# The delta rule's solve emitted in 12 steps between halves of a stream's weights, and the retention's gates directly behind the retention

## The chip, the cores and the metric

The kernel runs on one core of a Trainium2 chip. The metric is device time in microseconds (us) from the start to the end of one execution; the median of three executions is used. A profile of one execution shows what each engine did: PE (matmuls), PEld (its weight loads), DVE (vector engine), ACT (scalar engine), POOL, and the DMA queues, of which SP issues all that matter here.

## The reference

One layer on 256 rows of width 2048, in float32: a mixer of two branches, cross-attention into 256 memory rows, an MLP. The mixer is where the change lies. All its inputs are columns of one product `h @ w_in`:

- Retention, 8 heads: q and k with rotary angles, scores times a decay, scores times v, a group norm, then `silu(rg) * yr`.
- Delta rule, 16 heads in chunks of 64: q, k, v through a short causal convolution and silu; then

```
m = where(strict, (k*beta) @ k.T * decay, 0)
t = triangular_solve(eye + m, eye)      # the elimination
u = t @ (v*beta);  w = t @ (k*beta*exp(cum_g))
v_new = u - w @ state                   # the solve, chunk after chunk
o = (q*exp(g)) @ state + (q @ k.T * decay) @ v_new
```

  followed by a norm of each head and `silu(gz) * yg`.
- The merge: `sigmoid(gate_a) * yr + sigmoid(gate_b) * yg`, then `@ w_out`.

So each branch has a silu gate and a sigmoid gate, four blocks of columns of `w_in`: RG and TA for the retention, GZ and TB for the delta rule.

## The kernel before

Every float32 product with weights is made of three products of rounded parts: a weight piece is fetched as 1 MB (`raw`, three buffers), and for each half of it (512 KB) ACT makes the rounded part `whi` (L95) and DVE the rest `wlo` (L96), three buffers each. A "half" below is such a half of a fetch. `blocks` (L174, L175) produces two blocks of 128 feature rows from two fetches, `chunk` (L136 to L138) a piece of 512 columns from four fetches. Both leave their result in PSUM, and a function given by the caller takes it out.

The mixer works in four groups of two retention heads and four delta-rule heads. `gdn_stream` computes q, k and v of a group's four heads, two heads at a time: three `blocks` with convolutions, then the gram matrices (L562 to L566) and the decayed matrices `alt`, the compact blocks `cmp_l` and the right sides `r4`. `gdn_core` has two parts. The elimination: `cmp_l` goes through DRAM (`scr_l`) into `lw`, 31 pairs of small DVE operations on 32 partitions (L619 product, L621 subtraction) invert it into `tw`, which goes through DRAM (`scr_t`, L623) and comes back in four pieces as `ct` (L626); DVE transposes it into `cu` (L628) and makes the block matrices `t` and `u` (L636, four operations each). The solve: 16 small matmuls (L646) make `am`; then nine products of eight 128x128 float32 matmuls each (L653), of which each needs the one before it, taken out of PSUM by ACT (`w`, L665; `y`, L668) or combined by DVE (`sq`, L666 and L667; `r`, L663); at the end the outputs (L677 to L680) and their norm into `yg` (L687).

`retention` computes q and k (two `blocks`), v (a `chunk`), the scores (L720, L721), their products with v (L106 to L108) and the normed `yr`. `gates` runs the chunks RG, TA (on `yr`), GZ, TB (on `yg`) and transposes the merge (L221).

The groups are chained by the loop at the end of the mixer: stream of group j, gates of group j-1, retention of group j, elimination and solve of group j. Nothing else is written out by hand: a scheduler goes through the program with an estimate of durations and places each instruction in its engine's queue by its place in the program's text, moved ahead by `tc.high_priority` (the fetches, and the taking out of PSUM), once its inputs and buffers are there. After that each engine runs its queue in order. Two pairs of PSUM banks (`s0`, `s1`) serve the weights, four banks (`b`) all else. `alt` has four buffers, one for each head of a group, `cmp_l` and `r4` one, and so the next group's first pair can take its gram matrices out only when the solve has read its own.

## Time and profile before

| | us |
|---|---|
| median of 3 executions | 2127.54 |
| lowest, highest | 2123.79, 2130.27 |
| the profiled execution | 2124.05 |
| its span, first to last instruction | 2122.3 |
| PE busy in it | 2088.8 |
| DVE busy | 1409.7 |
| ACT busy | 1091.6 |
| POOL busy | 29.7 |

The profile's page gives the whole, and the trace behind it can be asked for any stretch. In a row of the timeline stand the start, the duration, the engine, the line of the kernel, the operation and what it writes and reads; in square brackets the idle time of the engine before it and who ended it. In a row of the stretches stand its bounds, its length and then the busy time of PE, PEld, DVE, ACT and POOL with their numbers of instructions, the granted clock of PE as a share, the share of DMA and GB/s. The ends of matmuls are modelled, so that a short wait of PE behind a matmul can be shown as busy.

In time, the mixer's stretch goes from about 230 us to about 1125 us. The four eliminations end at 380.5, 509.8, 731.5 and 951.6 us, and the four solves (first L653 to last L653) stand at 392.5 to 408.9, 578.5 to 621.7, 801.3 to 844.5 and 1026.4 to 1077.3 us.

### The profile page before, as it was taken

Reading aid. Unit: us, or ns where it says so; the run is one execution under the profiler, and the core shown is the slowest. Engines: PE = TensorE matmul, PEld = TensorE weight load, DVE = VectorE, ACT = ScalarE, POOL = GpSimd, SP = SyncE. Lnnn points to the kernel's source line nnn. Section 1 sums busy time; section 2 is a strip of 40 time slices with the busy share of each in tenths; the row PEclk is TensorE's granted clock in tenths of the full one; section 3 lists DMA queues with packets and bytes.
Section 4 is the critical chain, followed back from the end, with each engine's and each line's share of the span. In section 5 each row is a group of like instructions: output and inputs, shape, how many; then the busy total and the mean of one; then the engine's idle time right before and its main releaser. Section 6 shows DMA issues by size and latency. Waiting matters only on the chain.

```text
span 2122.3 us, 28778 instructions
## 1 busy us (share of the span) xinstructions
PE 2088.8 (98%) x11172; PEld 1800.5 (85%) x11172; DVE 1409.7 (66%) x2225; ACT 1091.6 (51%) x1700; POOL 29.7 (1%) x39
## 2 busy tenths in 40 slices
PE   8999999799999999999999999999999999999998
PEld 6878888688898889888888899888888888888887
DVE  6756779578667876786557666666556656645655
ACT  7565565354556455645445555554434434434444
POOL 0000000000000000000000000000000000000000
PEclk9999999999999999999999999999999999999999
DMA  8777656355545654455457655566566556556653
GB/s 299 252 237 246 199 186 196 97 181 194 184 144 198 197 185 149 169 196 190 159 173 253 206 182 159 178 198 182 197 197 186 193 196 188 192 198 187 190 198 139
DMA packets 316009, 405.91 MB, mean 191 GB/s; under 512 B 16592, under 2 KB 224480, under 8 KB 315744
## 3 DMA queue, kind: packets, MB, share of 16 engines
q1 hardware_dynamic: 315872, 404.08, 58.9%
q8 instruction: 87, 1.43, 0.3%
q14 instruction: 50, 0.41, 0.1%
HBM read 390.40 MB, written 13.65 MB: 190 GB/s over the span
## 4 chain that ended last, share of the span: by engine, by line
PE 93%; DMA 3%; DVE 1%; ACT 1%; SPq 1%; issue 0%; POOL 0%; ACTq 0%; POOLq 0%; DVEq 0%
PE s L174 32%; PE s L175 16%; PE s L137 13%; PE s L138 13%; PE s L136 13%; PE b L653 2%; DMA row<-crow 1%; DMA xc<-x 1%; DMA dec_d<-dec_w 1%; DVE wlo L96 1%; PE b L564 0%; PE b L106 0%; DMA ct<-scr_t 0%; PE b L108 0%; PE b L107 0%
## 5 line engine op out<-in xcount | busy, mean ns | idle before, releaser
L96 DVE TENSOR_TENSOR wlo<-raw,whi 128x1024 fp32r<-128x1024 f32 x702 | 857.8, 1223 | 507.8 <-ACT whi L95 500.8
L95 ACT ACTIVATE whi<-raw 128x1024 fp32r<-128x1024 f32 x702 | 742.6, 1059 | 715.8 <-PE s L138 373.9
L174 PE MATMUL s<-q,whi 128*128 128x512 f32 x3088 | 1067.4, 392 | 1.2 <-DVE bo L180 0.9
L175 PE MATMUL s<-q,wlo 128*128 128x256 f32 x3088 | 847.3, 282 | 6.6 <-DVE wlo L96 6.6
L174 PEld LDWEIGHTS s<-q,whi 128*128 128x128 f32 x3088 | 573.2, 188 | 112.4 <-DVE bo L180 1.1
L175 PEld LDWEIGHTS s<-q,wlo 128*128 128x128 f32 x3088 | 580.9, 188 | 21.9 <-DVE wlo L96 10.6
L137 PE MATMUL s<-wlo,q 128*128 128x512 f32 x1264 | 494.1, 391 | 0.6 <-DVE wlo L96 0.6
L138 PE MATMUL s<-whi,q 128*128 128x512 f32 x1264 | 491.0, 389 | 0.0
L136 PE MATMUL s<-whi,q 128*128 128x512 f32 x1264 | 449.3, 390 | 0.1
L137 PEld LDWEIGHTS s<-wlo,q 128*128 128x128 f32 x1264 | 237.7, 188 | 49.6 <-DVE wlo L96 1.8
L136 PEld LDWEIGHTS s<-whi,q 128*128 128x128 f32 x1264 | 237.1, 188 | 49.7 <-ACT whi L95 0.5
L138 PEld LDWEIGHTS s<-whi,q 128*128 128x128 f32 x1264 | 237.5, 188 | 48.2
L179 ACT ACTIVATE bo<-s 128x256 f32<-128x256 f32 x193 | 73.0, 378 | 124.7 <-PE s L175 112.6
L180 DVE TENSOR_TENSOR bo<-bo,s 128x256 f32<-128x256 f32 x193 | 80.2, 416 | 47.2 <-ACT bo L179 47.1
L519 DVE SCALAR_TENSOR_TENSOR acc<-bo,cw,acc 128x255 f32<-128x255 f32 (+2 forms) x144 | 66.0, 477 | 2.8 <-ACT acc L516 1.8
L619 DVE TENSOR_TENSOR pr<-lw,tw 32x31 f32<-32x31 f32 (+15 forms) x124 | 40.4, 326 | 10.2 <-DMA lw<-scr_l 8.1
L621 DVE TENSOR_TENSOR tw<-tw,pr 32x31 f32<-32x31 f32 (+15 forms) x124 | 40.6, 328 | 2.5
L945 DVE SCALAR_TENSOR_TENSOR res<-s,rstd3q,res 128x512 f32<-128x512 f32 (+1 forms) x32 | 22.3, 735 | 11.8 <-PE s L138 11.8
L754 ACT ACTIVATE gth<-s 128x512 f32<-128x512 f32 x32 | 18.9, 590 | 18.7 <-PE s L138 15.5
L934 DVE SCALAR_TENSOR_TENSOR hs<-bo 128x256 f32<-128x256 f32 x64 | 27.0, 422 | 1.1
L937 DVE TENSOR_TENSOR q<-hs,q 128x256 fp32r<-128x256 f32 x64 | 26.8, 418 | 0.8 <-ACT q L936 0.8
L936 ACT ACTIVATE q<-hs 128x256 fp32r<-128x256 f32 x64 | 26.2, 410 | 0.0
(292 smaller groups left out, 1083.2 us busy)
## 6 DMA issues: line engine op xcount, KB each, us to landing
raw<-w_in SPq DMA_DIRECT2D x144, 1024.0 KB, 5.0
raw<-w_ff SPq DMA_DIRECT2D x128, 1024.0 KB, 5.4
raw<-w_xkv SPq DMA_DIRECT2D x31, 1024.0 KB, 5.9
raw<-w_out SPq DMA_DIRECT2D x16, 1024.0 KB, 5.8
raw<-w_xq SPq DMA_DIRECT2D x16, 1024.0 KB, 6.7
raw<-w_xo SPq DMA_DIRECT2D x16, 1024.0 KB, 5.3
dec_d<-dec_w SPq DMA_DIRECT2D x16, 192.0 KB, 4.7
dec<-dec_d SPq DMA_DIRECT2D x8, 384.0 KB, 3.2
```

The lines of the kernel that those rows point to most:

```text
L95: act.activation(hi, src, AF.Copy)
L96: vec.tensor_sub(lo, src, hi.bitcast(F32))
L136: pe.matmul(o, xh, wh, start=first, stop=False)
L137: pe.matmul(o, xh, wl, start=False, stop=False)
L138: pe.matmul(o, xl, wh, start=False, stop=last)
L174: pe.matmul(ps[b], lh, xhl, start=kk == 0, stop=False)
L175: pe.matmul(ps[b][:, :S], ll, xh, start=False, stop=kk == KT - 1)
L179: act.activation(o, ps[b][:, S:], AF.Copy)
L180: vec.tensor_add(o, o, ps[b][:, :S])
L519: vec.scalar_tensor_tensor(acc[:, d:], ps[:, :S - d], cw[:, j, blk:blk + 1], acc[:, d:], op0=ALU.mult, op1=ALU.add)
L621: vec.tensor_sub(tw[:, j + 1:32, 0:j + 1], tw[:, j + 1:32, 0:j + 1], pv)
L653: pe.matmul(pv[:, i, :], lhs(i), rhs[:, i, :], start=True, stop=True)
```

## The change

The elimination becomes a function of its own, `gdn_blocks`, called right behind the group's stream. The solve, `gdn_core`, becomes a generator that stops at 12 places: behind `am`, behind each product and its taking out, and behind each of the two outputs. A list `steps` holds the generator that runs. `chunk` and `blocks` call `step()` behind each half of their weights, so that one step of the solve is emitted there; `finish_steps()` empties the list where the next group's first pair needs its buffers. `cmp_l` and `r4` are allocated there instead of at the stream's start. `gates` is split: RG and TA run right behind the group's own retention, GZ and TB stay behind the next group's stream. In groups 1 to 3 the generator is put on the list before RG and TA, so that its steps stand between their halves; in group 0 behind them, so that its steps stand in the next group's stream.

The order of the work: before S0 R0 C0, S1 G0 R1 C1, S2 G1 R2 C2, S3 G2 R3 C3, G3 (S stream, R retention, C elimination and solve, G the four gates); now S0 E0 R0 A0, S1 with the steps of solve 0, E1 B0 R1 A1 with the steps of solve 1, S2 E2 B1 R2 A2 with those of solve 2, S3 E3 B2 R3 A3 with those of solve 3, B3 (E elimination, A the gates RG and TA, B the gates GZ and TB).

```diff
+    steps = []
+
+    def step():
+        if steps and next(steps[0], steps) is steps:
+            steps.pop(0)
+
+    def finish_steps():
+        while steps:
+            step()
...
                     for part in parts:
                         products(q, i, part, halves)
+                    if i % 2:
+                        step()
...
                     pe.matmul(ps[b][:, :S], ll, xh, start=False, stop=kk == KT - 1)
+                if i % (k // 2) == k // 2 - 1:
+                    step()
...
-        cmp_l = mx.tile([P, 8, 32], F32, name="cmp_l", tag="cmp", bufs=1)
-        r4 = mx.tile([P, 4, NT, GD], F32, name="r4", tag="r4", bufs=1)
...
                 blocks(h1, w_in[0], c0 + h0 * GD, 2, evac)
+            if pr == 0:
+                finish_steps()
+                cmp_l = mx.tile([P, 8, 32], F32, name="cmp_l", tag="cmp", bufs=1)
+                r4 = mx.tile([P, 4, NT, GD], F32, name="r4", tag="r4", bufs=1)
...
-    def gdn_core(grp, heads, cmp_l, r4, qe4, yg):
+    def gdn_blocks(heads, cmp_l):
...
+        return t0, u0, am
+
+    def gdn_core(t0, u0, am, heads, r4, qe4, yg):
...
             act.activation(am[:, :, t, :], pv, AF.Copy)
+        yield
...
             if t:
                 vec.tensor_sub(rhs, rhs, times(lambda i: heads[i][:, 0, P:S], y[:, :, 0, :]))
+                yield
             w, sq = tmp("w"), tmp("sq")
             act.activation(w, times(lambda i: am[:, i, t, :], rhs), AF.Copy)
+            yield
             vec.tensor_add(sq, rhs, times(lambda i: am[:, i, t, :], w))
+            yield
             vec.tensor_sub(sq, sq, times(lambda i: am[:, i, t, :], sq))
+            yield
             act.activation(y[:, :, t, :], times(lambda i: u0[:, i, t, :], sq), AF.Copy)
+            yield
...
+        def of_retention(j, yr):
+            chunk(h1, cols(w_in[0], C_RG + 512 * j), silu_gate(yr))
+            chunk(h1, cols(w_in[0], C_TA + 512 * j), sig_gate(yr))
+
+        def of_delta_rule(j, yr, yg, quad, before=None):
+            chunk(h1, cols(w_in[0], C_GZ + 512 * j), silu_gate(yg))
+            chunk(h1, cols(w_in[0], C_TB + 512 * j), sig_gate(yg, yr), before=before)
+            to_feature(lambda t, f: yg[:, t, f * P:(f + 1) * P], None, quad)
...
-            group = gdn_stream(j)
-        if prev is not None:
+            heads, cmp_l, r4, qe4 = gdn_stream(j)
+            solved = gdn_blocks(heads, cmp_l)
+        if j:
...
             else:
+                finish_steps()
                 quad = quad_a()
-            gates(j - 1, prev[0], prev[1], quad, take_back if j == 4 else None)
+            gate_delta_rule(j - 1, yr, yg, quad, take_back if j == 4 else None)
...
             retention(j, yr)
-            gdn_core(j, *group, yg)
-            prev = (yr, yg)
+            core = gdn_core(*solved, heads, r4, qe4, yg)
+            if j:
+                steps.append(core)
+            gate_retention(j, yr)
+            if not j:
+                steps.append(core)
```

Where the instructions now stand is seen in the engines' queues. First PE, in the mixer at the solve of group 0 (`alt` are the group's decayed matrices, `b` a PSUM bank, `s` the PSUM of a weight product, `q` the rows' part). Before:

```order
L174 MATMUL s_4052<-q,whi 128x512
L175 MATMUL s_4052<-q,wlo 128x256
L646 MATMUL b<-alt,t_3420 128x128 x8
L653 MATMUL b<-r_2097,am 128x128 x4
L653 MATMUL b<-w,am 128x128 x4
L653 MATMUL b<-sq,am 128x128 x4
L653 MATMUL b<-sq,u_3421 128x128 x4
L653 MATMUL b<-y,alt 128x128 x4
L653 MATMUL b<-r_2097,am 128x128 x4
```

The same solve on PE now, in three pieces of the queue (L667 was L646, L675 was L653, L187 and L188 were L174 and L175):

```order
L188 MATMUL s_3727<-q,wlo 128x256
L667 MATMUL b<-alt,t_2991 128x128 x8
L187 MATMUL s_3728<-q,whi 128x512
...
L187 MATMUL s_3727<-q,whi 128x512
L675 MATMUL b<-r_2415,am 128x128 x4
L188 MATMUL s_3727<-q,wlo 128x256
...
L187 MATMUL s_3864<-q,whi 128x512
L675 MATMUL b<-w,am 128x128 x4
L188 MATMUL s_3864<-q,wlo 128x256
```

Before, the nine products of group 0's solve stood one behind the other with nothing between; now 23 to 31 rows of weight products stand between two of them. (The program's `x4` and `x8` are twice as many rows in the trace, since each float32 matmul is recorded as two.) In groups 1 and 2 they stood apart by 23 to 29 rows of `blocks` before, and by 22 to 25 of `chunk`, some with `blocks` behind, now; in group 3 by 22 to 27 rows of `chunk` before and 22 to 25 now.

Second DVE, in the mixer at the end of an elimination, here that of group 2, the third (`tw` the inverse, `ct` its way back through DRAM). Before:

```order
L96 TENSOR_TENSOR wlo<-raw,whi 128x1024
L619 TENSOR_TENSOR pr<-lw,tw 32x31
L621 TENSOR_TENSOR tw<-tw,pr 32x31
L96 TENSOR_TENSOR wlo<-raw,whi 128x1024
L613 MEMSET tw 32x1024
L614 MEMSET tw 32x32
L96 TENSOR_TENSOR wlo<-raw,whi 128x1024 x2
L628 STREAM_TRANSPOSE cu<-ct 128x256
L636 TENSOR_TENSOR t_7512<-ct,bd_658 128x256 x4
L636 TENSOR_TENSOR u_7513<-cu,bd_658 128x256 x4
L96 TENSOR_TENSOR wlo<-raw,whi 128x1024 x2
```

The same elimination on DVE now (L107 was L96, L636 and L638 were L619 and L621, L645 was L628, L653 was L636; `st` are the retention's scores, L752 and L753 were L724 and L725):

```order
L107 TENSOR_TENSOR wlo<-raw,whi 128x1024
L636 TENSOR_TENSOR pr<-lw,tw 32x60
L638 TENSOR_TENSOR tw<-tw,pr 32x2x30
L636 TENSOR_TENSOR pr<-lw,tw 32x31
L638 TENSOR_TENSOR tw<-tw,pr 32x31
L752 TENSOR_TENSOR st<-b,dm 128x256
...
L645 STREAM_TRANSPOSE cu<-ct 128x256
L653 TENSOR_TENSOR t_6780<-ct,bd_658 128x256 x4
L752 TENSOR_TENSOR st<-b,dm 128x256
L753 TENSOR_TENSOR st<-b,dm 128x128
L653 TENSOR_TENSOR u_6781<-cu,bd_658 128x256 x4
L107 TENSOR_TENSOR wlo<-raw,whi 128x1024
```

The elimination has moved from the stretch of the four gates to the end of the retention's products, so that its last pairs and the making of `t` and `u` now stand among the retention's scores; three halves' `wlo` stand between its last subtraction and `cu`, as before (four in groups 0 and 1; before three in all but group 3, which had four). The elimination of group 3 stands in the same way.

Third SP, at the way back of the same elimination. Before:

```order
L85 DMA raw<-w_in 128x8x256
L623 DMA scr_t<-tw 32x1024
L626 DMA ct<-scr_t 32x8x32 x2
L85 DMA raw<-w_in 128x8x256
L626 DMA ct<-scr_t 32x8x32 x2
```

Now (L96 was L85, L640 was L623, L643 was L626):

```order
L96 DMA raw<-w_in 128x4x512 x5
L640 DMA scr_t<-tw 32x1024
L643 DMA ct<-scr_t 32x8x32
L96 DMA raw<-w_in 128x4x512
L643 DMA ct<-scr_t 32x8x32 x3
L746 DMA dm<-dm_d 128x256
```

One of the four pieces instead of two is now issued ahead of the next 1 MB of weights, three behind it, in groups 2 and 3; in group 0 it was one and is two, in group 1 it was two and is three. In groups 2 and 3 the decay matrix `dm` of the retention's second head now stands behind the pieces too.

More of the change, by code (lines that the diff above doesn't have):

```diff
@@ L657, in tmp @@
             return mx.tile([P, 4, GD], F32, name=nm, tag="g_" + nm, bufs=1)
-        y = big("y", "g_a")
+        y = mx.tile([P, 4, NT, P], F32, name="y", tag="g_a", bufs=1)
         for t in range(NT):
@@ L688, in gdn_core @@
                                          gdng, op0=ALU.mult, op1=ALU.mult)
+            yield
     def retention(j, yr):
@@ L748, in retention, with gates @@
             vec.tensor_mul(yr[:, t, :], yr[:, t, :], gng)
-    def gates(j, yr, yg, quad, before=None):
+    def gates():
         def gate_of(ps, f, scale):
@@ L769, in sig_gate @@
             return evac
-        chunk(h1, cols(w_in[0], C_RG + 512 * j), silu_gate(yr))
-        chunk(h1, cols(w_in[0], C_TA + 512 * j), sig_gate(yr))
-        chunk(h1, cols(w_in[0], C_GZ + 512 * j), silu_gate(yg))
-        chunk(h1, cols(w_in[0], C_TB + 512 * j), sig_gate(yg, yr), before=before)
-        to_feature(lambda t, f: yg[:, t, f * P:(f + 1) * P], None, quad)
+        def of_retention(j, yr):
[5 more added lines that the diff above has]
+            to_feature(lambda t, f: yg[:, t, f * P:(f + 1) * P], None, quad)
+        return of_retention, of_delta_rule
     kept, merged = [], []
@@ L784, in take_back @@
             merged.append(back)
-    prev = None
+    gate_retention, gate_delta_rule = gates()
     for j in range(5):
         if j < 4:
-            group = gdn_stream(j)
-        if prev is not None:
+            heads, cmp_l, r4, qe4 = gdn_stream(j)
+            solved = gdn_blocks(heads, cmp_l)
+        if j:
             if j < 4:
```

## The prediction

> **What bounds the kernel now.** The page comes first: what share of the span PE works, and what the chain that ended last is made of; its last line here is DVE's conversion of weights, 1.22 us for a half.
>
> ```profile
> span 2122.3 us, 28778 instructions
> PE 2088.8 (98%) x11172; PEld 1800.5 (85%) x11172; DVE 1409.7 (66%) x2225; ACT 1091.6 (51%) x1700; POOL 29.7 (1%) x39
> PE 93%; DMA 3%; DVE 1%; ACT 1%; SPq 1%; issue 0%; POOL 0%; ACTq 0%; POOLq 0%; DVEq 0%
> L96 DVE TENSOR_TENSOR wlo<-raw,whi 128x1024 fp32r<-128x1024 f32 x702 | 857.8, 1223 | 507.8 <-ACT whi L95 500.8
> ```
>
> PE bounds the kernel; the change takes no matmul away, so it can win only time in which PE stands still or runs slowly. Next the stretches of the mixer, to see where PE stands still (the second and third number are length and PE busy).
>
> ```profile
> 240.00:420.00 180.00, 169.17 (x981) 147.81 (x980) 140.12 (x298) 95.56 (x173) 8.95 (x7) 0.99 0.51 163
> 860.00:1080.00 220.00, 220.00 (x1098) 186.63 (x1098) 154.34 (x256) 110.28 (x163) 3.41 (x4) 1.00 0.55 182
> 1080.00:1240.00 160.00, 160.00 (x896) 139.82 (x895) 109.25 (x156) 88.62 (x134) 2.71 (x3) 1.00 0.67 211
> ```
>
> 180.00 less 169.17 is 10.83 us of idle PE in the first row, none in the two others. The mixer's first group has the hole, the later ones have not. The timeline of PE shows what it is:
>
> ```profile
> 394.34 1.16 PE L653 MATMUL b<-w,am 128*128 128x128 f32 x8 [0.69 <-ACT w L665]
> 396.28 1.16 PE L653 MATMUL b<-sq,am 128*128 128x128 f32 x8 [0.78 <-DVE sq L666]
> 416.67 0.39 PE L566 MATMUL b<-kh 128*128 128x256 f32 x1 [1.42 <-DVE yg L687]
> 418.20 0.80 PE L174 MATMUL s<-q,whi 128*128 128x512 f32 x1 [0.92 <-DVE bo L180]
> 418.80 0.41 PE L175 MATMUL s<-q,wlo 128*128 128x256 f32 x1
> 419.01 0.63 PE L174 MATMUL s<-q,whi 128*128 128x512 f32 x1
> 583.60 1.05 PE L653 MATMUL b<-w,am 128*128 128x128 f32 x8
> 584.41 0.36 PE L175 MATMUL s<-q,wlo 128*128 128x256 f32 x1
> 584.97 0.39 PE L174 MATMUL s<-q,whi 128*128 128x512 f32 x1
> 585.20 0.28 PE L175 MATMUL s<-q,wlo 128*128 128x256 f32 x1
> 585.31 0.39 PE L174 MATMUL s<-q,whi 128*128 128x512 f32 x1
> ```
>
> In group 0 each product of the solve waits for the one before it to be taken out: 1.94 us from 394.34 to 396.28. In group 1 the same eight rows cost 0.81 us (583.60 to 584.41), with weight products ahead and behind. And behind group 0's solve a weight product lasts longer: the L174 at 419.01 0.63 us, that at 584.97 0.39. The granted clock says why:
>
> ```profile
> 323.28:432.61 109.33, 98.50 (x575) 85.90 (x574) 83.07 (x181) 52.03 (x99) 6.94 (x5) 0.97 0.44 140
> 561.67:654.42 92.75, 92.75 (x576) 82.97 (x575) 67.20 (x124) 51.37 (x99) 4.41 (x5) 1.00 0.49 158
> 784.45:877.20 92.75, 92.75 (x576) 82.97 (x575) 67.20 (x124) 51.36 (x99) 4.41 (x5) 1.00 0.49 158
> 417.50:424.20 6.70, 6.00 (x19) 5.13 (x20) 6.30 (x19) 4.01 (x14) 1.01 (x1) 0.50 0.18 59
> ```
>
> The last row has a clock of 0.50. The first three are the measure of the whole: each goes from a group's second L721 to the first matmul of the next gates, and holds the same work, the end of the retention, one solve and the next stream (575 and 576 matmuls). It takes 109.33 us around group 0's solve and 92.75 around the two others.
>
> **What the change removes.** Now group 0's products stand 23 to 31 weight rows apart, as in groups 1 and 2 of before, so its stretch should cost what theirs does: 109.33 - 92.75 = 16.6 us less. Of that, 10.83 is idle PE, about 3.0 the half clock (418.2 to 424.2 at half speed does 3.0 us of work), and the rest, some 2.8, waits that modelled ends hide (products shown as busy for 1.16 us that cost 0.81 elsewhere, nine times).
>
> The cover holds: 23 rows are 11.5 pairs of 0.34 us (584.97 to 585.31), 3.9 us; the result needs 0.81 on PE, 0.7 to 0.8 on ACT or DVE (the idle times above), and stands behind at most one conversion of 1.22 us, 2.8 together. Without that cover a product would cost the 1.94 - 0.81 = 1.1 us again.
>
> The moved gates RG and TA are 8 MB of weights with their conversions and taking-out, the same instructions on PE, ACT, DVE and SP at another place. I cost them at nothing: group 3 of before already has RG right behind its own retention and its solve between their halves, and its rows above (860 to 1080, 1080 to 1240) show no idle PE. What waits then is `yr`, at RG's end, eight halves later.
>
> **What it adds: the way back of the elimination.** Before, group 1's to 3's eliminations end during the gates, and `am` follows much later. Now they end just ahead of `am`, among the retention's scores. DVE waits in order at `cu` for `ct`, and behind it stand `wlo` (PE's weights) and, now, `t` for PE's L646. The four waits of before, from the last subtraction to `cu`, and what the third cost:
>
> ```profile
> 380.34 0.18 DVE L621 TENSOR_TENSOR tw<-tw,pr 32x31 f32<-32x31 f32 x1
> 389.18 0.45 DVE L628 STREAM_TRANSPOSE cu<-ct 128x256 f32<-128x256 f32 x1 [0.92 <-DMA ct<-scr_t]
> 509.58 0.18 DVE L621 TENSOR_TENSOR tw<-tw,pr 32x31 f32<-32x31 f32 x1
> 519.27 0.44 DVE L628 STREAM_TRANSPOSE cu<-ct 128x256 f32<-128x256 f32 x1 [1.65 <-DMA ct<-scr_t]
> 731.32 0.18 DVE L621 TENSOR_TENSOR tw<-tw,pr 32x31 f32<-32x31 f32 x1
> 735.41 1.23 DVE L96 TENSOR_TENSOR wlo<-raw,whi 128x1024 fp32r<-128x1024 f32 x1
> 738.13 1.23 DVE L96 TENSOR_TENSOR wlo<-raw,whi 128x1024 fp32r<-128x1024 f32 x1 [1.49 <-ACT whi L95]
> 742.12 0.45 DVE L628 STREAM_TRANSPOSE cu<-ct 128x256 f32<-128x256 f32 x1 [2.77 <-DMA ct<-scr_t]
> 742.49 1.39 DVE L636 TENSOR_TENSOR t<-ct,bd 128x256 f32<-128x256 f32 x4
> 951.38 0.18 DVE L621 TENSOR_TENSOR tw<-tw,pr 32x31 f32<-32x31 f32 x1
> 963.59 0.45 DVE L628 STREAM_TRANSPOSE cu<-ct 128x256 f32<-128x256 f32 x1 [1.46 <-DMA ct<-scr_t]
> 746.41 0.51 PE L175 MATMUL s<-q,wlo 128*128 128x256 f32 x2 [0.77 <-DVE wlo L96]
> 432.61:546.34 113.73, 113.73 (x546) 95.59 (x545) 89.84 (x162) 57.68 (x80) 1.01 (x1) 1.00 0.59 196
> 654.42:769.10 114.68, 113.91 (x546) 95.49 (x545) 88.68 (x160) 56.69 (x79) 1.01 (x1) 1.00 0.58 192
> 877.20:990.84 113.64, 113.64 (x546) 95.59 (x545) 87.48 (x158) 56.69 (x79) 1.01 (x1) 1.00 0.58 190
> ```
>
> The way back r is 8.7, 9.5, 10.6 and 12.0 us (742.12 less 731.50, the subtraction's end). A half lasts 2.72 (735.41 to 738.13). Gates and retention of the same work (the last three rows) take 113.7, 114.68 and 113.64: the third elimination, with three halves between and r = 10.6, cost PE 1.0 us; those with shorter waits nothing.
>
> - Groups 2 and 3 now: three halves again; the last subtraction is one pair later in its half (two operations of about 0.2: 0.4), two `st` stand between `t` and `u` (0.42 + 0.28, by the row of L724 and L725 below, 0.65 with overlap), and elimination and retention crowd DVE there, which I put at 0.5 (0 to 1.5; DVE is busy 89.84 of 113.73). So 1.6 later at the same r: the cost is r - 10.6 + 1.0 + 1.6 = r - 8.0 each. `dm`, which one `st` needs, is issued behind `ct` and has t's 1.39 us to land.
> - Group 1: four halves between, but PE's L646 asks for `t` itself. By the queues' order, with DVE two halves ahead of PE, it comes 4.5 halves and the retention's 16 products (256 columns, 0.11 each, as 585.20 to 585.31) behind the `wlo` that the elimination's end follows: 12.2 + 1.8, with the scores some 14.4 us. The subtraction ends 1.3 us into that half and 0.5 by crowding, `t` is ready r + 1.75 later (742.12 to 742.49 + 1.39). Cost r - 10.9.
> - Group 0: the same with 0.3 in place of 1.8, and L646 at 14.7: r - 12.7.
>
> ```profile
> L724 DVE TENSOR_TENSOR st<-b,dm 128x256 f32<-128x256 f32 x8 | 3.4, 419 | 4.7 <-PE b L721 4.4 <-DMA dm<-dm_d 0.3
> L725 DVE TENSOR_TENSOR st<-b,dm 128x128 f32<-128x128 f32 x8 | 2.2, 281 | 0.0
> ```
>
> The four together, less the 1.0 of before: at r = 8.7, 1.4 - 1.0 = 0.4; at 10.0, 4.0 - 1.0 = 3.0; at 12.0, 1.1 + 4.0 + 4.0 - 1.0 = 8.1. I take 10.0, between 9.5 and 10.6, the two rows whose subtraction stands at the same place against the fetches as groups 2 and 3 have it now (in the second half of one).
>
> **The sum.** -16.6 + 3.0 = -13.6 us. The profiled execution's 2124.05 becomes 2110.5; it lies 3.5 below the median of 2127.54, which becomes 2113.9. I predict 2114.
>
> [...]
>
> **The rivals.**
>
> *The half clock does not come from the hole.* Then it stays or comes elsewhere: 3.0 us less won, 2113.9 + 3.0 = 2117. For it: single short waits ahead of it. Against: it begins at 417.5, at the hole's end, and the two equal stretches without a hole have a clock of 1.00. [...]
>
> *The way back is long at all sites,* r = 12: 16.6 - 8.1 = 8.5 won, 2119. For it: three of four pieces of `ct` now stand behind 1 MB of weights in groups 2 and 3. Against: group 0 of before had that order, at r = 8.7.
>
> *The hole only moves:* group 0's stream still runs dry, as `alt` and `kq` free late; each product costs 1.1 again and the clock falls. Nothing won, 2127. Against: the queue shows weight rows between all products.
>
> *Slower: SP's queue.* In groups 2 and 3 the weights between the first `ct` and the other three must wait for a buffer, and a buffer comes free with a `wlo` that stands behind DVE's work. If `scr_t` and `ct` each land behind a full transfer, r is 12.0 + 5.0 = 17.0 (5.0 is the landing of 1 MB):
>
> ```profile
> raw<-w_in SPq DMA_DIRECT2D x144, 1024.0 KB, 5.0
> ```
>
> The four then cost 4.3 + 6.1 + 9.0 + 9.0 - 1.0 = 27.4, or 10.8 net: 2138. It decides from r = 14.3 on, where the four make up the 16.6. Against: the longest r seen is 12.0, with the subtraction right behind a fetch's issue.
>
> **How the numbers follow.** The forecast (r from 8.7 to 11, 16.2 to 11.5 us won) has 0.74; the half clock that stays 0.06; the long way back 0.10; the hole that moves 0.06; slower 0.04. What a measurement here can tell from no change is about 0.3%, 6.4 us. Faster by more: the first two and most of the third, 0.88; within: the fourth and some of the third, 0.08; slower 0.04. The likeliest's own range is 2111 to 2116 by its terms; executions of before lie up to 3.8 us from their median, and the long way back ends at 2119: 2106 to 2120.
>
> **What would show it.** In the profile after: the stretch around group 0's solve as long as the others', about 92.8 us, no L653 with idle time of 0.7 ahead of it, no clock of 0.50 near 420; L653 rows about 4 to 5 us apart in all groups. At `cu`: idle DVE of 1 to 3 us, and behind it PE waiting for `wlo` or for `t` at L646 by 0 to 2 us in groups 1 to 3. Waits at L646 of over 4 us would show the way back mis-sized; a clock of 0.50 behind one of them, a loss that I have left out of the sum. A gain of more than 17 us would mean that the moved gates give something that I have costed at nothing.

## The result and the profile after

| | before | after |
|---|---|---|
| median, us | 2126.78 | 2106.83 |
| lowest, highest | 2123.79, 2130.27 | 2105.39, 2107.15 |
| executions | 4 | 4 |
| the profiled execution | 2124.05 | 2106.88 |

After takes 0.9908 of the time of before, with a 95% interval of 0.9892 to 0.9925: 16 to 23 us less, 20.0 by the medians and 17.2 by the two profiled executions. The time of before is now that of four executions, the three of the prediction and one more, so its median differs a little from the one there.

The edit moved line numbers. Of the lines spoken of, L174 and L175 (weight products of `blocks`) are now L187 and L188, L136 to L138 (of `chunk`) L147 to L149, L628 (`cu`) L645, L636 (`t`, `u`) L653, L653 (the solve's products) L675, L566 (gram matrices) L583.

From the page of after: the span, the busy times, and the chain that ended last.

```profile
span 2105.2 us, 28781 instructions
PE 2083.3 (99%) x11172; PEld 1796.9 (85%) x11172; DVE 1407.7 (67%) x2225; ACT 1091.6 (52%) x1700; POOL 28.7 (1%) x39
...
PE 93%; DMA 3%; ACT 2%; DVE 1%; SPq 1%; issue 0%; ACTq 0%; POOLq 0%; POOL 0%; DVEq 0%
```

The work is the same, 11172 matmuls; PE is still the bound, and the 17.1 us of span that went are time in which it stood still or ran slowly.

To see where, one needs stretches that hold the same work in both kernels. The prediction's stretches around a solve no longer do, since RG and TA moved across their bounds. From the last scores of one group to the last scores of the next it is the same work: one solve, one stream, four gates, one retention, 1187 to 1189 matmuls. These are the three such cycles of before, as stretches (bounds, length, then the busy time of PE, PEld, DVE, ACT and POOL, the granted clock, DMA share, GB/s):

```profile
323.28:561.67 238.39, 227.56 (x1189) 194.23 (x1188) 183.06 (x357) 118.42 (x190) 7.94 (x6) 0.99 0.52 171
561.67:784.45 222.78, 222.01 (x1189) 191.21 (x1188) 166.04 (x298) 116.77 (x189) 5.42 (x6) 1.00 0.54 179
784.45:1006.19 221.74, 221.74 (x1189) 191.31 (x1188) 164.85 (x296) 116.76 (x189) 5.42 (x6) 1.00 0.54 178
```

And of after:

```profile
323.30:544.95 221.65, 221.65 (x1188) 191.26 (x1187) 177.68 (x343) 117.92 (x190) 6.81 (x6) 1.00 0.55 182
544.95:766.75 221.80, 221.80 (x1187) 191.27 (x1186) 166.12 (x303) 116.28 (x188) 5.59 (x6) 1.00 0.55 180
766.75:988.50 221.75, 221.75 (x1187) 191.25 (x1186) 164.62 (x296) 116.88 (x189) 5.42 (x6) 1.00 0.54 178
```

The first cycle is 16.74 us shorter, the second 0.98, the third the same: 17.7 together. In all three PE is now busy for the whole length, at a clock of 1.00. Outside of them the profiled executions differ by 0.5 the other way: 0.8 us longer behind the last cycle, and 0.3 shorter ahead of the first scores, which start at 322.94 in after (its four bounds above lie some 0.3 us behind the start of the scores). Other profiles of these kernels scatter by as much.

The hole of group 0 is gone. The products of its solve in the timeline of PE:

```profile
385.29 0.40 PE L187 MATMUL s<-q,whi 128*128 128x512 f32 x1
385.53 1.05 PE L675 MATMUL b<-r,am 128*128 128x128 f32 x8
386.34 0.36 PE L188 MATMUL s<-q,wlo 128*128 128x256 f32 x1
...
390.36 0.39 PE L187 MATMUL s<-q,whi 128*128 128x512 f32 x1
390.59 1.05 PE L675 MATMUL b<-w,am 128*128 128x128 f32 x8
391.40 0.36 PE L188 MATMUL s<-q,wlo 128*128 128x256 f32 x1
```

A product starts 5.06 us behind the one before it, with weights between, and costs 0.81 us (385.53 to 386.34), as in the later groups of before.

That leaves what the prediction had as the price, the way back of the elimination. From the timeline of DVE in after: the last subtraction of each of the four eliminations, and the row at `cu` that follows it.

```profile
365.39 0.17 DVE L638 TENSOR_TENSOR tw<-tw,pr 32x31 f32<-32x31 f32 x1
...
377.91 0.45 DVE L645 STREAM_TRANSPOSE cu<-ct 128x256 f32<-128x256 f32 x1 [1.56 <-DMA ct<-scr_t]
...
546.93 0.18 DVE L638 TENSOR_TENSOR tw<-tw,pr 32x31 f32<-32x31 f32 x1
...
558.91 0.45 DVE L645 STREAM_TRANSPOSE cu<-ct 128x256 f32<-128x256 f32 x1 [1.23 <-DMA ct<-scr_t]
...
759.68 0.18 DVE L638 TENSOR_TENSOR tw<-tw,pr 32x31 f32<-32x31 f32 x1
...
768.35 0.44 DVE L645 STREAM_TRANSPOSE cu<-ct 128x256 f32<-128x256 f32 x1
...
981.49 0.18 DVE L638 TENSOR_TENSOR tw<-tw,pr 32x31 f32<-32x31 f32 x1
...
990.16 0.44 DVE L645 STREAM_TRANSPOSE cu<-ct 128x256 f32<-128x256 f32 x1
```

The way back r is 12.3, 11.8, 8.5 and 8.5 us. DVE waits in groups 0 and 1 (1.56 and 1.23 us), not in groups 2 and 3. PE waits for none of it: the trace shows no idle time of PE of more than 0.1 us between 323 and 988 us.

So two questions were left. The change has three parts: the solve in steps, the gates RG and TA behind the retention, the elimination directly behind the stream. Which of them closes the hole? And why did the way back cost nothing?

### The profile page after: what moved, and what is told of

Its sections match the earlier page's. It is cut to its first block, busy times and chain, and to the rows that moved or that the text cites. A ratio compares the mean times of both kernels' runs of the same rounds, so it can differ in the third digit from the quotient of the medians.

```text
span 2105.2 us, 28781 instructions
## 1 busy us (share of the span) xinstructions
PE 2083.3 (99%) x11172; PEld 1796.9 (85%) x11172; DVE 1407.7 (67%) x2225; ACT 1091.6 (52%) x1700; POOL 28.7 (1%) x39
## 4 chain that ended last, share of the span: by engine, by line
PE 93%; DMA 3%; ACT 2%; DVE 1%; SPq 1%; issue 0%; ACTq 0%; POOLq 0%; POOL 0%; DVEq 0%
PE s L187 32%; PE s L188 17%; PE s L148 13%; PE s L149 13%; PE s L147 13%; PE b L675 2%; DMA dec_d<-dec_w 1%; ACT whi L106 1%; DVE wlo L107 1%; ACT dec_w L493 1%; PE b L581 1%; DMA xc<-x 1%; PE b L117 0%; DMA xt_d<-xt 0%; PE b L119 0%; PE b L118 0%
## 5 line engine op out<-in xcount | busy, mean ns | idle before, releaser
L107 DVE TENSOR_TENSOR wlo<-raw,whi 128x1024 fp32r<-128x1024 f32 x702 | 858.3, 1223 | 522.0 <-ACT whi L106 516.2
L187 PE MATMUL s<-q,whi 128*128 128x512 f32 x3088 | 1063.4, 390 | 0.7 <-ACT whi L106 0.4
L188 PE MATMUL s<-q,wlo 128*128 128x256 f32 x3088 | 845.3, 281 | 5.2 <-DVE wlo L107 5.1
L187 PEld LDWEIGHTS s<-q,whi 128*128 128x128 f32 x3088 | 570.8, 188 | 111.5 <-ACT whi L106 1.6
L188 PEld LDWEIGHTS s<-q,wlo 128*128 128x128 f32 x3088 | 579.0, 188 | 20.1 <-DVE wlo L107 8.8
L149 PE MATMUL s<-whi,q 128*128 128x512 f32 x1264 | 492.4, 390 | 0.0
L147 PE MATMUL s<-whi,q 128*128 128x512 f32 x1264 | 454.1, 391 | 0.0
L147 PEld LDWEIGHTS s<-whi,q 128*128 128x128 f32 x1264 | 237.5, 188 | 49.2 <-ACT q L249 0.4
L149 PEld LDWEIGHTS s<-whi,q 128*128 128x128 f32 x1264 | 237.6, 188 | 48.0
L636 DVE TENSOR_TENSOR pr<-lw,tw 32x31 f32<-32x31 f32 (+15 forms) x124 | 40.4, 325 | 8.4 <-DMA lw<-scr_l 6.5
L638 DVE TENSOR_TENSOR tw<-tw,pr 32x31 f32<-32x31 f32 (+15 forms) x124 | 40.5, 327 | 2.1
L984 DVE SCALAR_TENSOR_TENSOR res<-s,rstd3q,res 128x512 f32<-128x512 f32 (+1 forms) x32 | 22.3, 735 | 11.8 <-PE s L149 11.8
L531 ACT ACTIVATE acc<-bo,cw 128x256 f32<-128x256 f32 x48 | 24.1, 503 | 4.5 <-DVE bo L195 4.4
```

Source lines behind the costliest of these rows:

```text
L107: vec.tensor_sub(lo, src, hi.bitcast(F32))
L147: pe.matmul(o, xh, wh, start=first, stop=False)
L149: pe.matmul(o, xl, wh, start=False, stop=last)
L187: pe.matmul(ps[b], lh, xhl, start=kk == 0, stop=False)
L188: pe.matmul(ps[b][:, :S], ll, xh, start=False, stop=kk == KT - 1)
L638: vec.tensor_sub(tw[:, j + 1:32, 0:j + 1], tw[:, j + 1:32, 0:j + 1], pv)
```

## The experiments

Theory A is the prediction's: the steps put weights between the products. Theory B: the moved gates do it, which the prediction costed at nothing. The expectations below use these names where they were at stake.

### The steps without the moved gates

From after; the gates stand where they stood before, and the elimination comes behind the retention again.

```diff
-            solved = gdn_blocks(heads, cmp_l)
         if j:
+            gate_retention(j - 1, yr)
...
             retention(j, yr)
-            core = gdn_core(*solved, heads, r4, qe4, yg)
-            if j:
-                steps.append(core)
-            gate_retention(j, yr)
-            if not j:
-                steps.append(core)
+            solved = gdn_blocks(heads, cmp_l)
+            steps.append(gdn_core(*solved, heads, r4, qe4, yg))
```

> The change without the move of the gates: RG and TA stand behind the next stream as before, the elimination behind the retention as before, and every group's solve is emitted in its 12 steps in the next stream (the last group's in its gates). Theory A, that the emission in steps takes group 0's solve apart: the stretch around it shrinks from 109.3 to about 93 us, some 2110 us. Theory B, that the moved gates do it, since they give 16 halves of weights (44 us) while the elimination runs and the scheduler takes a solve apart by itself wherever weights are left: nine products of group 0 one behind the other as before, the hole and its 16.6 us stay, 2124 to 2128 us.

Measured: 2128.67 us (10 executions, 2122.51 to 2132.80) beside 2127.70 of before (13 executions); the ratio is 1.0002 (0.9990 to 1.0014). No change. Its first cycle among the stretches, and the start of its solve in the timeline of PE:

```profile
327.58:567.87 240.29, 229.30 (x1188) 195.63 (x1187) 183.47 (x357) 118.93 (x190) 7.94 (x6) 0.98 0.54 170
```

```profile
398.88 1.16 PE L675 MATMUL b<-w,am 128*128 128x128 f32 x8 [0.69 <-ACT w L688]
400.81 1.16 PE L675 MATMUL b<-sq,am 128*128 128x128 f32 x8 [0.78 <-DVE sq L690]
402.75 1.16 PE L675 MATMUL b<-sq,u 128*128 128x128 f32 x8 [0.78 <-DVE sq L692]
```

The hole is there whole, 1.94 us from product to product. The solve is emitted in twelve steps between halves of weights, and stands in PE's queue in one piece all the same, as in before. Theory A falls.

### The moved gates without the steps

From after; the solve is emitted in one piece, and the elimination stands behind the retention. Of the three parts only the move of RG and TA is left. (`cmp_l` and `r4` stay at their new place in this run and in the one before it, which shows that this place alone gives nothing.)

```diff
-            solved = gdn_blocks(heads, cmp_l)
...
             retention(j, yr)
-            core = gdn_core(*solved, heads, r4, qe4, yg)
-            if j:
-                steps.append(core)
+            solved = gdn_blocks(heads, cmp_l)
+            for _ in gdn_core(*solved, heads, r4, qe4, yg):
+                pass
             gate_retention(j, yr)
-            if not j:
-                steps.append(core)
```

> The change without steps: RG and TA directly behind the group's own retention, but elimination and solve emitted in one piece between the two, as in the kernel before. Theory A: the hole stays, 2124 to 2128 us. Theory B: as the changed kernel, 2105 to 2108 us, the stretch from one group's scores to the next group's 221.6 to 222 us in all groups.

Measured: 2107.54 us (2103.83 to 2108.64), ratio 0.9902 (0.9885 to 0.9918), against 0.9908 of the whole change. Its cycles:

```profile
325.81:547.61 221.80, 221.80 (x1188) 191.31 (x1187) 178.61 (x343) 117.99 (x190) 7.99 (x6) 1.00 0.58 183
547.61:769.31 221.70, 221.70 (x1189) 191.31 (x1187) 166.09 (x303) 116.13 (x189) 5.59 (x6) 1.00 0.57 180
769.31:990.93 221.62, 221.62 (x1189) 191.32 (x1187) 164.28 (x296) 116.96 (x189) 5.43 (x6) 1.00 0.57 178
```

All three are as long as those of after. The moved gates give the whole gain, and the steps and the early elimination add nothing to it that the intervals can tell. What the gates do is seen from where the weights of the next stream stand. These are the stretches with the instructions of L174 alone (PE busy with it, its number), in before: up to the solve, during it, and behind it.

```profile
323.28:392.30 69.02, 54.23 (x160) 1.00 0.63 201
392.30:416.60 24.30, 0.00 (x0) 1.00 0.05 14
416.60:432.61 16.01, 13.76 (x32) 0.79 0.22 71
```

And with L187 alone in after: up to the solve, during it, and behind; then, in this run, up to the solve and during it.

```profile
323.30:385.20 61.90, 6.75 (x20) 1.00 0.56 187
385.20:430.00 44.80, 36.92 (x105) 1.00 0.51 165
430.00:445.00 15.00, 10.05 (x29) 1.00 0.49 158
```

```profile
325.81:388.10 62.29, 6.82 (x20) 1.00 0.60 192
388.10:433.00 44.90, 37.01 (x105) 1.00 0.53 165
```

A stream has 192 of them. In before, group 0's elimination ends at 380.5 and the solve is ready at 392, 69 us behind the scores; by then PE has done 160 of the 192. The last 32 could not start: the first of them waits for `bo`, the taking out of an earlier `blocks` (L174 at 418.20 in the prediction's rows), and ACT's part of that (L179) waits at 415.28 and 417.66 for `dj` (L570), which DVE makes from the gram matrices behind the solve. So nothing that was ready was left to put between the products. In after, PE does RG and TA first (16 halves of 2.72 us, some 44 us), so that only 20 of the 192 are done when the solve is ready, and the scheduler spreads the products among 105 others, by itself, whether they come in steps or not: in this run, without steps, the counts are the same. The elimination itself also ends sooner with the gates moved, 42.6 us behind the start of the scores in after and 42.8 in this run, against 57.2 in before and with the steps alone. What makes it faster was not tested; the early elimination was not run by itself, but by these numbers it is not what does it.

### One of the two gates

As the run with the moved gates alone, with TA left at its old place: half the cover.

```diff
         def of_retention(j, yr):
             chunk(h1, cols(w_in[0], C_RG + 512 * j), silu_gate(yr))
+
+        def of_ta(j, yr):
             chunk(h1, cols(w_in[0], C_TA + 512 * j), sig_gate(yr))
...
+            gate_ta(j - 1, yr)
             gate_delta_rule(j - 1, yr, yg, quad, take_back if j == 4 else None)
```

> As the run with the gates alone, but only RG moves and TA stays behind the next stream: 8 halves (22 us) of weights instead of 16. By the queue's order six of group 0's nine products then stand apart and the last three stand one behind the other with the outputs. Theory B: a smaller hole, three products at 1.1 us and the waits at its end of about 3 us, with or without a stretch of half clock (3 us): 6 to 10 of the 16.6 us stay, 2113 to 2118 us. Theory A: 2124 to 2128 us.

Measured: 2114.05 us (2112.96 to 2114.82), ratio 0.9938 (0.9923 to 0.9953). The first two cycles, the end of the solve in the timeline of PE, and the stretches of L187 alone up to the solve and during it:

```profile
322.44:555.38 232.94, 228.21 (x1201) 195.82 (x1200) 184.49 (x358) 118.93 (x191) 7.99 (x6) 0.99 0.56 176
555.38:774.17 218.79, 218.79 (x1176) 189.05 (x1175) 164.68 (x297) 115.66 (x188) 5.54 (x6) 1.00 0.57 181
```

```profile
418.79 1.16 PE L675 MATMUL b<-sq,am 128*128 128x128 f32 x8 [0.78 <-DVE sq L690]
420.72 1.16 PE L675 MATMUL b<-sq,u 128*128 128x128 f32 x8 [0.78 <-DVE sq L692]
...
429.62 0.38 PE L583 MATMUL b<-kh 128*128 128x256 f32 x1 [1.44 <-DVE yg L714]
```

```profile
322.44:385.60 63.16, 29.16 (x86) 1.00 0.60 190
385.60:422.00 36.40, 26.54 (x75) 1.00 0.56 174
```

A few weight rows crossed from the second cycle into the first (1201 and 1176 matmuls), so the three go together: 673.3 us, 8.0 more than after's, 9.6 less than before's. Eight halves of cover take away somewhat more than half of the loss. The elimination ends as early as in after (42.8 us behind the scores), but 86 of the 192 are done when the solve starts: 75 others spread its first products, and the last two still wait 0.78 us each. The half clock stays for 6.8 us, as in before. The loss goes by the weights that are left, as theory B has it.

### The moved gates in group 0 alone

From after; as with the moved gates alone, but in groups 1 to 3 RG and TA stay behind the next stream.

```diff
+            if j > 1:
+                gate_retention(j - 1, yr)
             gate_delta_rule(j - 1, yr, yg, quad, take_back if j == 4 else None)
...
-            gate_retention(j, yr)
             if not j:
-                steps.append(core)
+                gate_retention(j, yr)
```

> As the run with the gates alone, but RG and TA move in group 0 alone; groups 1 to 3 have the order of before. If the whole gain is group 0's hole, 16.6 us less than before: about 2110 us, with the 0.9 us at the third elimination as before. If the other groups' order gives something of its own, it lies nearer to before by that.

Measured: 2108.95 us (2107.62 to 2112.06), ratio 0.9916 (0.9902 to 0.9931). Its first two cycles:

```profile
326.58:548.38 221.80, 221.80 (x1189) 191.30 (x1187) 178.49 (x343) 117.84 (x190) 7.99 (x6) 1.00 0.58 183
548.38:772.36 223.98, 222.09 (x1189) 191.24 (x1187) 169.08 (x312) 116.02 (x189) 5.43 (x6) 1.00 0.57 179
```

Group 0 gives nearly all. What remains is the second cycle: 2.2 us longer than in after, with 1.9 us of idle PE, the wait for the third elimination that before has too (1.0). So in groups 1 to 3 the moved gates are worth 1 to 2 us, since that elimination no longer stands where PE waits for its way back; by the medians this is not more than the intervals can tell.

### A longer way back

From after; `tw` goes through DRAM once more.

```diff
-        nc.sync.dma_start(scr_t, tw.rearrange("p i c -> p (i c)"))
+        scr_t0 = dram.tile([32, 1024], F32, name="scr_t0", tag="scr_t0", bufs=2)
+        nc.sync.dma_start(scr_t0, tw.rearrange("p i c -> p (i c)"))
+        nc.sync.dma_start(scr_t, scr_t0)
```

> The changed kernel with the inverse of each elimination copied once more through DRAM (128 KB) on its way back, all four pieces of ct then behind the next 1 MB of weights. The order on PE and DVE is that of the changed kernel. The way back, 12.3, 11.8, 8.4 and 8.5 us in the changed kernel, grows by 3 to 6 us. By the prediction's terms (r - 12.7, r - 10.9, r - 8.0, r - 8.0) at 16, 16, 13 and 13 us: 3.3 + 5.1 + 5.0 + 5.0 = 18 us more than the changed kernel, some 2125. By the slack that the changed kernel's trace shows (costs from r = 13.0, 12.6, 9.8 and 9.8 on): 3.0 + 3.4 + 3.2 + 3.2 = 13 us, some 2120. If the wait at cu is hidden anyway: 2107.

Measured: 2106.51 us (2104.91 to 2107.74), ratio 0.9912 (0.9895 to 0.9928): no cost. The extra transfer lengthened r by only 1.0 to 1.4 us, less than expected, to 13.8, 13.1, 9.5 and 9.6. PE's order is that of after; on DVE two `st` of groups 2 and 3 stand a few rows earlier. DVE's idle time ahead of `cu` grew, in all and in group 0, as the costliest groups and the timeline of DVE show:

```profile
L647 DVE STREAM_TRANSPOSE cu<-ct 128x256 f32<-128x256 f32 x4 | 1.8, 446 | 6.0 <-DMA ct<-scr_t 6.0
```

```profile
378.36 0.45 DVE L647 STREAM_TRANSPOSE cu<-ct 128x256 f32<-128x256 f32 x1 [2.99 <-DMA ct<-scr_t]
```

The same group has 2.8 us in after. None of the 3.2 more reaches PE: the cycles are 221.63, 221.84 and 221.81. By the prediction's terms these r would have cost 1.1, 2.2, 1.5 and 1.6 us. They cost nothing, so its onsets of 12.7, 10.9 and 8.0 (the r from which PE would wait) lie too early.

### The way back three transfers longer

The same with three more.

```diff
-        nc.sync.dma_start(scr_t, tw.rearrange("p i c -> p (i c)"))
+        hop = tw.rearrange("p i c -> p (i c)")
+        for n in range(3):
+            nxt = dram.tile([32, 1024], F32, name=f"scr_t{n}", tag=f"scr_t{n}", bufs=2)
+            nc.sync.dma_start(nxt, hop)
+            hop = nxt
+        nc.sync.dma_start(scr_t, hop)
```

> The changed kernel with three more copies through DRAM on the way back of each elimination. Here the scheduler's queues differ: in group 0 the 16 matmuls that make am stand two halves (31 rows of weight products, 5.4 us) later on PE, since it plans with an estimate of each transfer. The way back grows by some 4 to 6 us, to 17, 17, 13 and 13. If the places of before held, the prediction's terms would give 4.3 + 6.1 + 5.0 + 5.0 = 20 us more, some 2127. If the planned places move with the way and hide it: no stretch from scores to scores over 223 us, some 2107.

Measured: 2113.27 us (1 execution; before on the same chip 2125.54). r is 19.6, 18.2, 16.9 and 16.4 us. The cycles are 226.55, 222.52 and 221.78: 5.6 us more than after's. By the prediction's terms it would have been 6.9 + 7.3 + 8.9 + 8.4 = 31.5. Group 0, in the timeline of DVE and of PE, and PE's clock in a stretch:

```profile
386.31 0.45 DVE L650 STREAM_TRANSPOSE cu<-ct 128x256 f32<-128x256 f32 x1 [3.40 <-DMA ct<-scr_t]
```

```profile
451.59 0.50 PE L187 MATMUL s<-q,whi 128*128 128x512 f32 x1 [2.34 <-DVE bo L195]
```

```profile
452.10:455.50 3.40, 3.40 (x12) 2.92 (x12) 3.40 (x9) 2.41 (x9) 0.00 (x0) 0.50 0.26 89
```

DVE stood 3.40 us at `cu`, and PE had no wait there: the scheduler had put `am` 31 weight rows later. What it cost came some 60 us later, where the late solve ends close to the stream's end and DVE works off its outputs (L719, 1.13 us at 446.12) just ahead of the stream's own `wlo`, `dj` and `bo`: one wait of 2.34 us for `bo`, and a window of half clock behind it. That the late solve is what holds `bo` up there is read from this order, not tested. So the way back does have a price, but in group 0 it begins above 13.8 us, and it showed at the stream's end, not at the place where the prediction looked for it. The third cycle, with r = 16.9 at its start, is as long as in after.

### The way back by another queue

From after; the writing of `scr_t` and the four pieces of `ct` go by POOL's queue, past SP's weights.

```diff
-        nc.sync.dma_start(scr_t, tw.rearrange("p i c -> p (i c)"))
+        nc.gpsimd.dma_start(scr_t, tw.rearrange("p i c -> p (i c)"))
...
-            nc.sync.dma_start(ct[32 * q:32 * q + 32], ...)
+            nc.gpsimd.dma_start(ct[32 * q:32 * q + 32], ...)
```

> The changed kernel with the way back of the elimination (scr_t and ct) issued by POOL instead of SP, so that nothing in SP's queue stands between its parts. If the place in SP's queue makes the way back long in groups 0 and 1 (12.3 and 11.8 us), it falls to about the 8.4 of the others; if the transfer of weights that is already under way does, it stays near 12. The time: no change from 2107 in either case, since PE waits for none of the four now.

Measured: 2105.42 us (1 execution), r 12.0, 12.8, 10.2 and 10.4 us, cycles 221.64, 221.84 and 221.81. Out of SP's queue the way back is hardly shorter in group 0, and in the three others 1 to 2 us longer. Whether POOL's queue has a cost of its own was not tested, so this run alone does not clear SP's. The times of issue say more. In after the first `ct` was issued 5.2 and 4.6 us behind `scr_t` in groups 0 and 1, where a fetch of weights had been issued 0.5 and 1.0 us ahead of it, and 2.0 and 2.1 us behind it in groups 2 and 3, where the last fetch lay 3.3 us back. With POOL's queue `scr_t` landed 5.4, 4.4, 2.2 and 3.4 us behind its issue. A fetch that is already under way fits both; it is read from the order, not tested.

### A third buffer for the decay rows

A profiled execution of one kernel differs from another's mostly ahead of the first scores, which come at 321 to 328 us, and there DVE waits between 120 and 170 us for the decay rows. From after, with three row buffers in place of two.

```diff
-        row = kv.tile([P, S], F32, name="row", bufs=2)
+        row = kv.tile([P, S], F32, name="row", bufs=3)
...
```

The part left out lets the constant `zer` share the buffers of `em`.

> The changed kernel with three buffers instead of two for the decay rows, for whose landing DVE waits in order between 120 and 170 us (12 waits, 17 us), ahead of wlo. That stretch is where executions of one kernel differ: from the start to the first group's scores 322.4 to 327.6 us in the profiles so far. If the second buffer is what makes the rows late: 2 to 4 us less, 2103 to 2105. If the row's own transfer does, no change, 2107.

Measured: 2106.17 us (2105.28 to 2108.41), ratio 0.9910 (0.9895 to 0.9924), first scores at 322.97. No gain: the second buffer is not what holds the early part. The clock also fell to 0.50 between 140 and 175 us in some profiles: for 3.4 us in before, here and in two others, for 6.8 with the moved gates alone and for 10.2 with the steps alone, and not at all in after.

### The solve's products twice

From before; in group 0 each product is computed a second time into another bank, so that PE is busy for twice as long between the waits. If the waits between products bring the half clock, it should go.

```diff
+            if grp == 0:
+                again = bank().rearrange("p (h n) -> p h n", h=4)
+                for i in range(4):
+                    pe.matmul(again[:, i, :], lhs(i), rhs[:, i, :], start=True, stop=True)
```

> The kernel before with each of group 0's nine products done a second time into another bank, right behind the first; nothing reads the second. PE then works through most of the time in which a product is taken out, and the chain is not longer, since the second takes 0.85 us where the wait was about 1.1. If the waits between products bring the half clock behind the solve: no clock of 0.5 near 420, the first stretch from scores to scores 3.0 us shorter, 235.4 instead of 238.4. If the waits at the solve's end (1.6, 1.1, 1.0 us) bring it, or the price is not 3.0: 238.4 as before.

Measured: 2126.85 us (1 execution; before 2126.20). The first cycle and two pieces of it as stretches, and a wait in the timeline of PE:

```profile
321.18:564.76 243.58, 236.31 (x1261) 203.53 (x1260) 182.86 (x357) 118.46 (x190) 7.95 (x6) 0.98 0.53 167
389.40:392.80 3.40, 3.29 (x16) 3.00 (x15) 3.13 (x7) 0.50 (x2) 0.00 (x0) 0.50 0.35 136
420.10:426.90 6.80, 5.88 (x19) 4.85 (x18) 6.44 (x19) 3.58 (x12) 1.01 (x1) 0.50 0.17 53
```

```profile
389.11 3.58 PE L646 MATMUL b<-alt,t 128*128 128x128 f32 x16 [2.43 <-DVE t L636]
```

The half clock near 420 stays for 6.8 us, though of the nine waits between products only three remain (0.26, 0.78 and 0.78 us). Right ahead of it stand waits of 0.82 and 1.29 us at the gram matrices behind the solve. So in this window it is these that bring it, and not those between the products. The cycle's length missed both expectations: 5.2 us more than before's, in which an additional window of half clock at 389.4, behind a wait of 2.43 us for `t`, has a share. The rest stays open.

### A short elimination

From before; its expectation says what is left out. Gates, steps and order are those of before; only the solve of group 0 is ready early.

```diff
-        for j in range(31):
+        for j in range(31 if grp else 10):
```

> The kernel before, but group 0's elimination stops after 10 of its 31 pairs (its inverse is then incomplete; all else is computed as before). Gates, steps and order of the program as before. If the hole is there because the elimination is done only when few weights are left ahead of the next group's buffers: the solve becomes ready some 45 us earlier, stands among the next stream's weights, and the first stretch from scores to scores falls from 238.4 to 222 us without any gate moved, some 2110 us. If the order of the program makes the hole: 238.4 as before.

Measured: 2109.29 us (1 execution). The first cycle, and the stretches of L174 alone up to the solve, during it and behind it:

```profile
324.04:546.61 222.57, 221.96 (x1188) 191.19 (x1187) 170.92 (x315) 116.89 (x190) 5.43 (x6) 1.00 0.58 182
```

```profile
324.04:345.50 21.46, 9.63 (x28) 1.00 0.65 199
345.50:391.40 45.90, 38.19 (x109) 1.00 0.53 161
391.40:417.00 25.60, 19.66 (x56) 1.00 0.46 149
```

The solve is ready at 345 us, when 28 of the 192 are done; it stands among 109 others, and the hole and the half clock are gone, with no gate moved and no step. So it is the relation that counts, how late the solve is ready against how many weights are left, and not the gates as such. In a kernel that must do all 31 pairs the gates are one way to set it; by this run a faster elimination would be another.

## Why the prediction was right, and where it was wrong

The sign and the size of the main term were right, the part of the change that it was credited to was not, and the cost set against it did not come.

- **What the change removes.** 16.6 us were forecast, from stretches of equal work; the first cycle became 16.74 shorter. The working of the size holds: the hole goes, the half clock in it goes, and group 0's cycle becomes as long as the others. What happens on PE holds too: the order of after's queue was read rightly (products 23 to 31 weight rows apart), and weight rows between the products cover their waits. Which part of the change puts them there was not asked. Both parts were in that order, and by setting the gates to nothing the prediction left the credit to the steps. The failed step is "The moved gates RG and TA ... I cost them at nothing": alone they give 0.9902, the steps alone 1.0002.
- **What shows in before that it could not be the steps.** In groups 1 to 3 of before the solve already stands spread among weights, from a text in one piece. The prediction used this as the measure of what group 0 would cost, without asking why the same text was not spread in group 0. The 160 of 192 weight products in the row above are the answer, and they were in the trace of before.
- **The way back.** +3.0 us were forecast, -1.0 was measured (the wait of the third elimination went, and no other came): the sum is off by 4 us here. r was taken as 10.0 at all sites; it was 12.3 and 11.8 in groups 0 and 1, 8.5 in groups 2 and 3. With these the prediction's terms give 0 + 0.9 + 0.5 + 0.5 - 1.0 = +0.9, so of the 4.0 some 2.1 come from r and 1.9 from the onsets. Runs with r up to 13.8 cost nothing at all, and one at 16.4 to 19.6 cost 5.6 where the terms say 31.5 - 1.0. Part of why is seen with the longer way back: in groups 0 and 1 `t` is taken head by head (group 0's `am` starts at 379.39, its fourth `t` ends at 380.12), and the first head's `t` is ready 0.28 and 0.44 us before `am` starts. From these rows the onsets there are near 14.1 and 13.6, an estimate for this order of the queues. In groups 2 and 3 `am` stands 7.5 us and more behind the first head's `t`; how long a way back `wlo` would bear there was not measured. The mis-sized step in groups 0 and 1 is the place of `am`: the prediction had it 14.7 (without a working) and 14.4 us behind the start of the `wlo` that the elimination's end follows; in after it is 16.1 and 16.5 (364.25 to 380.38 and 544.93 to 561.44).
- **The sum.** 13.6 us less were forecast; the profiled executions give 17.2, the medians 20.0. The forecast of 2113.9 is 7.1 too high: 4.1 from the three cycles (17.7 against 13.6), less 0.5 outside of them, and 3.5 because the profiled execution of before lay 3.5 below the median then known, and that of after lies at its own. The prediction carried that distance over to after. That the measured 2106.83 lies in the range of 2106 to 2120 is in part luck: it lies outside the 2111 to 2116 of the prediction's terms, and 2111 less the 3.8 of scatter is 2107.2, so that only the wider lower bound, for which no working stands, holds it. What makes executions of before scatter more (2123.79 to 2130.27 against 2105.39 to 2107.15) was not settled; that a hole leaves room for one window of half clock more or less, as between before and the steps alone, would fit, and is only argued.
- **The rival with a half clock that stays** is out: no clock below 1.00 in any cycle of after. The hole and the half clock near its end went together in each kernel that closed the hole; where half of the cover was left, the half clock stayed whole.
- **The rival with a long way back at all sites** had the right size of r for groups 0 and 1, and no cost. **The rival by SP's queue** is out: its r of 17 did not come (8.5 to 12.3), and in the run whose r came near it (16.4 to 19.6) the kernel still took 2113.3, 12 us less than before.
- **The rival that the hole only moves** did not come with the whole change, whose queue had weights between the products. What it describes came with the steps alone, the part that the forecast left the credit to.
- **What would show it.** No idle time ahead of the solve's products and no clock of 0.50 near 420: as said. Products 4 to 5 us apart: 5.0 to 6.6. DVE idle 1 to 3 us at `cu`: in two of four groups. PE waiting up to 2 us in groups 1 to 3: not at all. And "a gain of more than 17 us would mean that the moved gates give something that I have costed at nothing": it came out so, for the larger reason that they give all of it.

## What to carry to other kernels

When a dependent chain stands in a hole at one place and spread at others, ask first what work was left for the scheduler to put between at each place: count it (here 160 of 192 weight products were gone when the chain became ready) before changing how the chain is written. Independent work moved ahead of the fillers, or a chain that is ready earlier, closes such a hole; cutting the chain into steps did nothing. And where a change has several parts, work out the order of the queues for each part alone before one of them gets the credit.

## What the runs showed of the hardware

**When the clock halved.** Between the first 15 us and the last 15 of the program, before has two stretches of half clock, after has none. Those of before and the pieces of 3.41 us around them, as stretches:

```profile
158.01:161.42 3.41, 1.25 (x8) 0.87 (x7) 2.31 (x4) 2.40 (x10) 0.00 (x0) 1.00 0.98 324
161.42:164.84 3.42, 3.42 (x12) 2.94 (x11) 0.60 (x2) 1.68 (x3) 0.00 (x0) 0.50 0.55 198
164.84:168.25 3.41, 3.10 (x17) 2.37 (x17) 2.43 (x3) 3.41 (x13) 0.00 (x0) 1.00 0.32 85
...
414.01:417.42 3.41, 1.86 (x10) 1.42 (x10) 2.04 (x13) 0.45 (x2) 1.01 (x1) 1.00 0.01 2
417.42:420.84 3.42, 2.64 (x8) 2.25 (x9) 3.35 (x12) 1.95 (x6) 1.01 (x1) 0.50 0.00 0
420.84:424.25 3.41, 3.41 (x13) 2.92 (x12) 3.03 (x9) 2.12 (x9) 0.00 (x0) 0.50 0.35 115
424.25:427.66 3.41, 3.41 (x23) 2.98 (x22) 1.40 (x4) 2.76 (x9) 0.00 (x0) 1.00 0.00 0
```

They last 3.41 and 6.83 us, and their starts lie 256.00 us apart, 75 times 3.413. In four other profiles stretches of the same lengths stand at the solve of group 0 or behind it: 3.4 and 6.8 us with the steps alone (from 412.9 and 423.1), 6.8 with one of the two gates (from 429.9), 3.4 and 6.8 with the products twice (from 389.4 and 420.1), 3.4 with three transfers more (from 452.1).

What PE did in the 3.41 us ahead of each is counted from the matmuls' starts, in pieces of 3.41 us laid from the start of a profile's stretch of half clock, each matmul at about its spacing at full clock (512 columns 0.22 us, all smaller ones 0.11); it is an estimate of PE's share from these rows. Ahead of half clock it was 0.27 and 0.40 in before (from 158.0 and 414.0), 0.40 and 0.39 with the steps alone (409.5 and 419.7), 0.37 with one of the two gates (426.5), 0.20 and 0.41 with the products twice (386.0 and 416.7), 0.22 with three transfers more (448.7). The lowest share at full clock that no half clock followed was 0.41 in before (396.9) and 0.44 in after (129.3). The two kinds meet at 0.41, nearer than this counting can tell, and what sets the clock was not tested. In holes of the same form, 1.94 us from product to product, the 3.41 us at 396.9 in before did not lead to half clock, and those at 409.5 with the steps alone did: holes alike in length cost one stretch more or less here.

In before a pair of L174 and L175 takes 0.64 us at half clock (419.01 to 419.65) and 0.35 behind it (425.57 to 425.92). So 3.41 us of half clock cost at most 3.41 x (1 - 0.35 / 0.64) = 1.5 us, an estimate from these rows.

**Several short waits were enough here.** In the eight pieces ahead of half clock named above, the longest single idle time of PE was 2.16 and 1.42 us in before, 0.78 and 1.76 with the steps alone, 1.44 with one of the two gates, 2.43 and 1.29 with the products twice, 2.34 with three transfers more. In the one with 0.78 us there are two such waits, ahead of the products at 410.38 and 412.32, and the clock fell to 0.50 at 412.9.

**A transfer more in a chain.** In groups 0 and 1, where DVE waits for the way back in all three kernels, one more transfer of 128 KB through DRAM lengthened it by 1.4 and 1.3 us, three more by 7.2 and 6.4. Each added transfer took 2.3 to 4.1 us there, from its issue to the next. The end became shorter: from the first `ct` issued to `cu` it was 6.7 us in group 0 of after, 5.7 with one transfer more and 4.8 with three more (7.1, 5.8 and 4.8 in group 1).
